# Shifted copies of two bias rows: from DRAM to DRAM by head on GpSimd's queue

## The chip, the core and the metric

The kernel runs on one core of a Trainium2 chip. The metric is the device time of one execution in microseconds (us). Before the change it is 3416.61 us, the median of 3 runs (3416.25 to 3418.32).

A core has five engines that run side by side and meet at semaphores: TensorE (PE, matmuls), VectorE (DVE), ScalarE (ACT), GpSimd (POOL) and SyncE (SP). Transfers are issued from queues, here SP's for the weights and GpSimd's for smaller things, and are carried by 16 DMA engines.

## The reference

Two transformer blocks over 512 tokens of 1024 channels. The first block has two layers, each a feed-forward, a mix of four kinds of attention and recurrence, and a second feed-forward; the second block has one layer of feed-forward, two attentions and feed-forward. Two of the attentions add a bias to the scores that depends only on the distance between query and key and on the head:

```python
def nsa_mixer(...):                      # first block, 4 heads, in both layers
    ...
    wl = einsum(qb, kwb) + t5_table[t5_bucket(wd)].transpose(2, 0, 1)
    o_w = einsum(masked_softmax(wl, wmask), vwb)
    ...

def dilated_window_attention(q, k, v, t5_bias, window, dilation):   # second block, 8 heads
    ...
    bias = t5_bias[:, t5_bucket_2(off * dilation)]
    s = where(valid, einsum(qs, k_blk) * HEAD_DIM ** -0.5 + bias[:, None], MASK_VALUE)
    ...
```

As the bias depends on the distance alone, a head needs one row of numbers, one for each distance. For 128 queries on 128 partitions the row is wanted 128 times, each copy shifted by one place.

## The kernel before, in words

Activations stay in SBUF, channels on partitions. All large products run in three passes on TensorE (`mm3`, lines 306 to 315): each operand is split in a high and a low part, and high x high (line 308), low x high (311) and high x low (312) are added up in PSUM. Weights come in chunks of 128 x 1024 (512 KB) through `wchunk` (lines 287 to 300): SP loads the chunk into one of four buffers named `raw` (line 289), ACT casts its halves into `hi` (line 296), VectorE subtracts to get `lo` (line 297). There are four buffers each for `hi` and `lo`, of half a chunk. A `raw` buffer is free for the next load when its second `lo` is made.

A feed-forward (`ffn`, line 669) turns through 22 pieces of its inner width. In each turn two chunks are loaded and multiplied (2 x 24 matmuls of 512 columns); ACT applies silu, VectorE multiplies into `u` (line 701), GpSimd makes the operands of the down projection, `uh` (line 708) and `ul` (line 711). These are read only after the 22 turns. In the first feed-forward of the kernel, loads for the modulation (`in_ada`, line 382) go through the same `raw` buffers and SP's queue.

The bias rows are made as a side work, given to `ffn` as the generator `side`: from the fourth turn on, one step of it is taken in each turn, between `uh` and `ul` (line 710). `setup_nsa` (line 521) runs in the first feed-forward of layer one, `setup_bias` (line 532) in the second feed-forward of layer two (weights `in_f2a`) and, for what is left, in the first feed-forward of the second block (`in_g1a`). Each makes its rows with a matmul against one-hot columns and then writes 128 equal copies of each row to a DRAM tensor: `nsa_d` of 4 x 128 x 640 (lines 529 and 530) and `dil_d` of 8 x 128 x 1024 (line 547), from 4 and 8 partitions of SBUF, on SP's queue, the one of the weights. The source of line 547, `lcd`, is itself a `raw` buffer (line 517). The attentions read `nsa_d` and `dil_d` back on GpSimd's queue with a row step of 639 and 1023 elements, which makes the shift (lines 1485 and 1710). `setup_bias` also prepares the table of the neighbourhood attention from DRAM to DRAM on GpSimd's queue: one broadcast `nrb_d` (line 534), three `t1_d` (538, shown as `t_d` in the rows), and 24 `nb_d` (551).

Instructions are emitted in the program's order and a scheduler sets the order on each engine; `dep(a, b)` adds that `a` stands behind `b`. DMA waits for what it reads and overwrites.

Of the kernel before, what the change touches and what calls it, by code (L numbers as in the profile page):

```python
# [9 lines left out]
F32 = mybir.dt.float32  # L10
# [17 lines left out]
# channel blocks of w_in that come out with channels on partitions, in the order they are computed  # L28
# [30 lines left out]
# columns of per-channel parameters  # L59
# [166 lines left out]
def _body(tc, nc, ctx, I, out):  # L226
# [16 lines left out]
    # ---- activation tables: the functions come in runs that one table serves  # L243
# [3 lines left out]
    def dep(a, b):  # L247
        tc.add_manual_dep(a.ins, b.ins.name, NOS, reason="table")
# [15 lines left out]
    # ---- small helpers  # L264
# [11 lines left out]
    class Parts(list):  # L276
        """columns in tiles of n"""
# [47 lines left out]
    # ---- constants and parameters  # L325
# [48 lines left out]
    # ---- conditioning: mod = silu(c) @ ada_w + ada_b, one third of a sublayer (1024 columns) at a time  # L374
# [36 lines left out]
    def mod_first():  # L411
        """the first norm, scale and shift, in two parts of the channels, with the first products between"""
# [96 lines left out]
    # ---- bias vectors of relative distances, kept in DRAM with one shifted copy per partition  # L509
    nsa_d = DR.tile([4, 128, 640], F32, name="nsa_d")  # L510
    dil_d = DR.tile([8, 128, 1024], F32, name="dil_d")
    nrb_d = DR.tile([16, 7680], F32, name="nrb_d")
# [8 lines left out]
    def setup_nsa():  # L521
        oh = bias_in("k_oh", 32, 640)
        yield
        r, ng = w_("r")[0:4], w_("ng")[0:4, 0:128]
        ps = psa()
        PE.matmul(ps[0:4, :], t5, oh[:, 0:512], start=True, stop=True)
        V.memset(ng, NEG)
        S.copy(r, ps[0:4, :])
        nc.sync.dma_start(nsa_d[:, :, 0:512], r.unsqueeze(1).to_broadcast([4, 128, 512]))
        nc.sync.dma_start(nsa_d[:, :, 512:640], ng.unsqueeze(1).to_broadcast([4, 128, 128]))  # L530

    def setup_bias():
        n = I["nrb"]
        i = nc.gpsimd.dma_start(nrb_d, bass.AP(n.tensor, n.offset, [[0, 16], [1, 7680]]))
        dep(i, order["ul"])
        for k, off in enumerate((0, -8, -16)):
            yield
            nc.gpsimd.dma_start(t1_d[k], bass.AP(nrb_d.tensor, nrb_d.offset + off + 31,
                                                 [[7679, 16], [960, 8], [64, 15], [1, 32]]))
        yield  # L540
        ohd, lcd = bias_in("k_ohd", 32, 1024), bias_in("k_lcd", 8, 1024)
        yield
        for h in range(2):
            ps = psa()
            PE.matmul(ps[0:8, :], t5b, ohd[:, h * 512:h * 512 + 512], start=True, stop=True)
            V.tensor_tensor(lcd[:, h * 512:h * 512 + 512], ps[0:8, :], lcd[:, h * 512:h * 512 + 512], op=ALU.add)
        nc.sync.dma_start(dil_d, lcd.unsqueeze(1).to_broadcast([8, 128, 1024]))
        yield
        for rr in range(8):
            for k in range(3):  # L550
                i = nc.gpsimd.dma_start(nb_d[:, rr * 16:rr * 16 + 16, k],
                                        t1_d[k, :, :, 7 - rr:15 - rr].rearrange("c h a b -> h c (a b)"))
                dep(i, order["ul"])
                yield

    # ---- norm over the channels of x, and the product's left operand in two parts
# [3 lines left out]
    class Stat:  # L560
        """(mean of the squares over the channels + EPS) ** -0.5 for each token, on all partitions"""
# [19 lines left out]
        def add_all(self):  # L581
            """of x, with the sums in two chains"""
            s = [self.s, self.r]
            p = self.p[0] = psa("st")
            for k in range(KD):
                q = s[k] if k < 2 else w_("sq")
                S.activation(q, xbox["x"][:, k], AF.Square)
                if 1 < k < KD - 1:
                    i = (V if k % 2 else G).tensor_tensor(s[k % 2], s[k % 2], q, op=ALU.add)
                    if k == 2:  # L590
                        dep(i, order["post"])
                    if k % 2 == 0:
                        order["aft"] = i
            for t in s:
                V.tensor_tensor(q, q, t, op=ALU.add)
            PE.matmul(p, ones, q, start=True, stop=True)
# [20 lines left out]
    def scaled(k, gain, sl):  # L617
        """x * gain; the norm's factor, the same for all channels of a token, is applied to the products"""
        xk, g = xbox["x"][:, k, sl], gain[:, k:k + 1]
        i = S.activation(hh[:, k, sl], xk, AF.Copy, scale=g)  # L620
        if sl.start == 0 and order["ev"]:
            dep(i, order["ev"][-1 if k >= KD // 2 else -2])
        run["cur"].append(i)
        V.scalar_tensor_tensor(hl[:, k, sl], xk, g, hh[:, k, sl].bitcast(F32), op0=ALU.mult, op1=ALU.subtract)  # L624

    # ---- A phase is a generator: it loads its first weights, multiplies them with each half of the tokens, does the
    # rest but its last products, and does these for each half; so the norm between two phases overlaps with both.
    evac = []

    def link(a, b, pre, early=False):  # L630
        """the end of phase a with the beginning of phase b; pre(h) makes half h of b's operand"""
# [15 lines left out]
    def first(ws):  # L647
        """the first chunks of a phase; needs the operand's tokens by halves"""
# [19 lines left out]
    # ---- feed-forward  # L668
# [70 lines left out]
    def wout_first(w, qs, cs, order, ns):  # L739
        """the first two chunks, with the parts ns of the contraction"""  # L740
# [52 lines left out]
    def rsq(o, i, scale, bias=None):  # L793
        """(scale * i + EPS) ** -0.5"""
        n = i.shape[0]
        act(o, i, AF.Ln, scale=scale, bias=epsc[0:n])
        act(o, o, AF.Exp, scale=-0.5)

    # ---- independent pieces of work are emitted in turn
# [12 lines left out]
    # ---- the four mixers of the first block  # L812
# [13 lines left out]
    def _mix1(l, MX, q0):  # L826
# [51 lines left out]
        def conv(t, v, n, cw):  # L878
            """causal depthwise convolution along the tokens"""
# [5 lines left out]
        # gated deltanet: short convolution and silu  # L885
# [17 lines left out]
        # compression of the keys and values of the first mixer  # L903
        hs = t_([128, 4, 32], "hs")

        def compress():
# [17 lines left out]
            # blocks as rows, those of the high parts and those of the low parts; the sum comes with the transpose  # L924
# [35 lines left out]
        # projections with tokens on partitions: values of the two others, and all gates  # L960
# [25 lines left out]
        # gates  # L986
# [6 lines left out]
        def softplus(o, xin, tmp):  # L993
            """o = max(xin, 0) + ln(1 + exp(-|xin|))"""
# [18 lines left out]
        def gates():  # L1013
            """silu and sigmoid of the output gates"""
# [31 lines left out]
    def sums(w, s, tiles):  # L1046
        """w^T s, in two passes with s in two parts, for a w of zeros and ones"""
# [33 lines left out]
    def gdn(blkr, l, MX, m_, n_, q_, s_, c_, t_, out_split, pr, cv, ga, beta, lvl):  # L1081
        kT, qT = [], []
        # decays
# [11 lines left out]
        # l2 norm of keys and queries  # L1095
# [15 lines left out]
        # (1 + B)^-1 by doubling the block size, for two heads at once: S keeps B of the head of parity 0, transposed, above  # L1111
        # the diagonal, and B of the other below. With X the lower inverse of the first head and Y the upper one of the
        # second's transpose, Z holds the blocks of X at even places and those of Y at odd places, and R the others.
# [3 lines left out]
        def sets(a, s):  # L1117
            """columns that stay in Z from a level to the next, and those that change places with R's"""
# [6 lines left out]
        # per chunk, heads in the order (parity, block)  # L1125
# [70 lines left out]
        # the recurrence over chunks  # L1196
# [81 lines left out]
    def mlstm(sel2, l, MX, m_, n_, q_, s_, c_, t_, out_split, pr, vd, gt, lf):  # L1278
        # running sums and maxima of the gates, heads on partitions; lf holds -log_sigmoid
# [84 lines left out]
    def soft_a(n_, s_, qh, kh, n, bias, nb=1):  # L1364
        """scores of 128 queries, exp(scores - max); the row sum comes with the values"""
# [12 lines left out]
    def soft_b(n_, t, n, o, vs):  # L1378
        """transpose of the weights, and their product with the values"""
# [11 lines left out]
    class Late:  # L1391
        """the second and third steps of a softmax, each some units behind the one before"""
# [18 lines left out]
    def nsa(blkr, l, MX, m_, n_, q_, s_, c_, t_, out_split, pr, hs, cw2, va, sg):  # L1411
        # compressed keys and values
# [22 lines left out]
        # norms of queries and keys  # L1435
# [46 lines left out]
        for h in range(4):  # L1482
# [3 lines left out]
            # compressed branch  # L1486
# [66 lines left out]
    # ---- the two attentions of the second block  # L1553
# [16 lines left out]
    def _mix2(MX, q0, wf):  # L1570
# [23 lines left out]
        # Scores take two passes: queries and keys in two parts each, high and low, and a product over the 128 rows  # L1594
        # (high, low) of a head's queries and (high, high) of its keys, then the high queries with the low keys.
# [190 lines left out]
    # ---- second block: residual with a norm after the product  # L1786
    gh = P.tile([128, 3, KD], F32, name="gh")

    def keep(g):
        """the product, scaled, in the place of x, which is in DRAM meanwhile"""  # L1790
# [7 lines left out]
    def post(h, gain=None):  # L1798
        """x += rmsnorm(y) * g, with y * g in the place of x; then the next phase's operand, or the end"""
# [24 lines left out]
    # ================================================================ program  # L1824
# [31 lines left out]
    def pre(h):  # L1856
        for k in range(KD):
            scaled(k, C("f1pre", 0, 8), HV[h])
# [25 lines left out]
```

## Time and profile before

| | |
|---|---|
| time, median of 3 | 3416.61 us |
| span of the profiled execution | 3414.4 us |
| PE busy | 3244.8 us (95%) |
| DVE busy | 1718.9 us (50%) |
| ACT busy | 1212.3 us (36%) |
| POOL busy | 732.8 us (21%) |
| weights' and SP's other transfers (q1) | 392.53 MB, 38.0% of 16 engines |
| GpSimd's transfers (q0) | 15.25 MB, 1.5% of 16 engines |

The span runs from the first to the last instruction of the profiled execution; the page gives no other time of it. Busy time counts instructions, and matmuls overlap, so PE's share says when PE had work, not how fast it did it. The share of a DMA queue is the time that its packets took, over 16 engines.

### The profile page before, as it was taken

The page shows a single profiled execution, that of the slowest core. Times are in us where ns is not written, and L with a number is a line of the kernel's source. Part 1 is how long each engine was busy: PE and PEld are TensorE (multiplying, and loading weights), DVE is VectorE, ACT ScalarE, POOL GpSimd, SP SyncE. Part 2 cuts the span into 40 slices and gives each one's busy share as a digit, 9 for nine tenths or more (in the row PEclk, how much of TensorE's full clock was granted, in tenths as well). Part 3 has the DMA queues.
Part 4 walks back from the last instruction along what each step waited for, and adds up shares of the span by engine and source line. Part 5 has one row for each costly group of instructions (what it writes and reads, how often), then busy time and mean ns, then how long its engine had stood idle before and what let it go on. Part 6 is the DMA issues. An engine that isn't in the chain of part 4 may idle for free.

```text
span 3414.4 us, 42938 instructions
## 1 busy us (share of the span) xinstructions
PE 3244.8 (95%) x16168; PEld 2690.2 (79%) x16168; DVE 1718.9 (50%) x2942; ACT 1212.3 (36%) x2287; POOL 732.8 (21%) x742
## 2 busy tenths in 40 slices
PE   7699999999999999999999992999999999999998
PEld 6488887778888888888777881888888877778887
DVE  6255576556555555537655530334443354554433
ACT  3122254454222232225445420233222345552232
POOL 3122222114222222212211420211221120131111
PEclk8899999999999999999999996999999999999999
DMA  6455642013555445534201335333333354443333
GB/s 229 106 177 162 194 147 89 29 41 129 166 167 168 152 150 173 158 116 143 87 29 41 114 106 73 115 107 109 110 103 95 106 170 114 116 125 98 99 96 103
DMA packets 133824, 410.73 MB, mean 120 GB/s; under 512 B 16073, under 2 KB 30025, under 8 KB 133345
## 3 DMA queue, kind: packets, MB, share of 16 engines
q1 hardware_dynamic: 128880, 392.53, 38.0%
q0 software_dynamic: 4592, 15.25, 1.5%
q8 instruction: 127, 2.08, 0.3%
q14 instruction: 81, 0.66, 0.1%
q10 hardware_dynamic: 144, 0.21, 0.0%
HBM read 374.07 MB, written 22.46 MB: 116 GB/s over the span
## 4 chain that ended last, share of the span: by engine, by line
PE 88%; DVE 4%; another core or an unknown queue 2%; DMA 2%; ACT 2%; issue 1%; POOL 1%; SPq 0%; DVEq 0%; ACTq 0%; POOLq 0%
PE m L308 14%; PE m L311 14%; PE m L312 14%; PE a L308 11%; PE a L312 11%; PE a L311 11%; PE o L1388 2%; PE pt L1382 1%; DMA raw<-in_f1a_dram 1%; DVE lo L297 1%; PE s L1700 1%; PE S L1328 1%; PE a L1182 1%; PE a L1166 1%
## 5 line engine op out<-in xcount | busy, mean ns | idle before, releaser
L297 DVE TENSOR_TENSOR lo<-raw,hi 128x512 fp32r<-128x512 f32 (+2 forms) x1056 | 803.6, 766 | 1008.2 <-ACT hi L296 985.5
L296 ACT CAST hi<-raw 128x512 fp32r<-128x512 f32 (+2 forms) x1056 | 638.7, 611 | 1742.6 <-PE m L311 885.7
L308 PE MATMUL m<-hh,hi 128*128 128x512 f32 (+1 forms) x1728 | 669.4, 387 | 78.0 <-ACT hi L296 66.8
L311 PE MATMUL m<-hl,hi 128*128 128x512 f32 (+1 forms) x1728 | 662.0, 383 | 5.6 <-DVE hl L624 4.3
L312 PE MATMUL m<-hh,lo 128*128 128x512 f32 (+1 forms) x1728 | 660.1, 382 | 1.7 <-DVE lo L297 1.7
L308 PE MATMUL a<-hh,hi 128*128 128x512 f32 (+1 forms) x1264 | 477.1, 377 | 32.9 <-ACT hi L296 32.9
L311 PE MATMUL a<-hl,hi 128*128 128x512 f32 (+1 forms) x1264 | 476.5, 377 | 1.0 <-DVE hl L614 1.0
L312 PE MATMUL a<-hh,lo 128*128 128x512 f32 (+1 forms) x1264 | 475.5, 376 | 0.0
L308 PEld LDWEIGHTS m<-hh,hi 128*128 128x128 f32 x1728 | 327.6, 190 | 141.6 <-ACT hi L296 67.3
L311 PEld LDWEIGHTS m<-hl,hi 128*128 128x128 f32 x1728 | 327.7, 190 | 66.8 <-DVE hl L624 5.4
L312 PEld LDWEIGHTS m<-hh,lo 128*128 128x128 f32 x1728 | 327.3, 189 | 64.9 <-DVE lo L297 5.6
L708 POOL TENSOR_SCALAR uh<-u 128x512 fp32r<-128x512 f32 x132 | 112.2, 850 | 1213.0 <-DVE u L701 820.9
L308 PEld LDWEIGHTS a<-hh,hi 128*128 128x128 f32 x1264 | 240.1, 190 | 76.2 <-ACT hi L296 33.8
L311 PEld LDWEIGHTS a<-hl,hi 128*128 128x128 f32 x1264 | 239.9, 190 | 44.8 <-DVE hl L614 1.8
L312 PEld LDWEIGHTS a<-hh,lo 128*128 128x128 f32 x1264 | 239.5, 189 | 43.5 <-DVE lo L297 1.0
L308 PE MATMUL a<-uh,hi 128*128 128x512 f32 (+1 forms) x660 | 229.6, 348 | 0.6
L311 PE MATMUL a<-ul,hi 128*128 128x512 f32 (+1 forms) x660 | 229.5, 348 | 0.0
L312 PE MATMUL a<-uh,lo 128*128 128x512 f32 (+1 forms) x660 | 228.7, 347 | 0.0
L308 PE MATMUL m<-uh,hi 128*128 128x512 f32 x528 | 205.8, 390 | 0.0
L312 PE MATMUL m<-uh,lo 128*128 128x512 f32 x528 | 205.4, 389 | 0.0
L311 PE MATMUL m<-ul,hi 128*128 128x512 f32 x528 | 205.4, 389 | 0.0
L711 POOL TENSOR_TENSOR ul<-u,uh 128x512 fp32r<-128x512 f32 x132 | 200.9, 1522 | 10.8
(460 smaller groups left out, 4002.1 us busy)
## 6 DMA issues: line engine op xcount, KB each, us to landing
raw<-in_ada_dram SPq DMA_DIRECT2D x144, 512.0 KB, 4.3
raw<-in_f1a_dram SPq DMA_DIRECT2D x88, 512.0 KB, 4.0
raw<-in_f2a_dram SPq DMA_DIRECT2D x88, 512.0 KB, 3.9
raw<-in_win_dram SPq DMA_DIRECT2D x48, 512.0 KB, 3.4
raw<-in_g1a_dram SPq DMA_DIRECT2D x44, 512.0 KB, 3.8
raw<-in_g2a_dram SPq DMA_DIRECT2D x44, 512.0 KB, 3.7
raw<-in_f1b_dram SPq DMA_DIRECT2D x32, 512.0 KB, 3.7
raw<-in_f2b_dram SPq DMA_DIRECT2D x32, 512.0 KB, 3.6
```

Source lines behind the costliest of these rows:

```text
L296: order["hi"] = S.copy(h, raw[:, s])
L297: order["lo"] = V.tensor_tensor(l, raw[:, s], h.bitcast(F32), op=ALU.subtract)
L308: i = PE.matmul(o, wh, xh, start=start, stop=False)
L311: PE.matmul(o, wh, xl, start=False, stop=False)
L312: j = PE.matmul(o, wl, xh, start=False, stop=stop)
L708: G.tensor_scalar(uh[:, j], u, 1.0, 0.0, op0=ALU.mult, op1=ALU.add)
L711: order["ul"] = G.tensor_tensor(ul[:, j], u, uh[:, j].bitcast(F32), op=ALU.subtract)
L1166: PE.matmul(p[:, bs_], B[:, bs_], Z[:, bs_], start=True, stop=True)
L1182: PE.matmul(p[:, bs_], RT[:, bs_], w[:, bs_], start=True, stop=True)
L1328: PE.matmul(ps[:, 0:n], dk[b][r, j * 128:j * 128 + 128], dq[b][r, j * 128:512], start=True, stop=True)
L1382: PE.transpose(pt[:, j * 128:j * 128 + 128], t[:, j * 128:j * 128 + 128], ident)
L1388: PE.matmul(o, r[:, j * 128:j * 128 + 128], v, start=j == 0, stop=j == len(vs) - 1)
```

## The change

Each row is first written once to a small DRAM tensor, `nsa_r` (4 x 640) or `dil_r` (8 x 1024), by SP. Then one transfer for each head, issued from GpSimd's queue, writes 128 copies of the row from there to `nsa_d[h]` (320 KB) or `dil_d[rr]` (512 KB). The four of `nsa_d` are issued one in each step of `side`, after one more empty step; the eight of `dil_d` stand ahead of every third `nb_d` transfer. Each stands behind the newest `ul`. The diff also takes out comments, which changes nothing; those parts are left out here.

```diff
@@ bias vectors of relative distances
     nsa_d = DR.tile([4, 128, 640], F32, name="nsa_d")
     dil_d = DR.tile([8, 128, 1024], F32, name="dil_d")
+    nsa_r = DR.tile([4, 640], F32, name="nsa_r")
+    dil_r = DR.tile([8, 1024], F32, name="dil_r")
...
@@ setup_nsa
         S.copy(r, ps[0:4, :])
-        nc.sync.dma_start(nsa_d[:, :, 0:512], r.unsqueeze(1).to_broadcast([4, 128, 512]))
-        nc.sync.dma_start(nsa_d[:, :, 512:640], ng.unsqueeze(1).to_broadcast([4, 128, 128]))
+        nc.sync.dma_start(nsa_r[:, 0:512], r)
+        nc.sync.dma_start(nsa_r[:, 512:640], ng)
+        yield
+        for h in range(4):
+            yield
+            i = nc.gpsimd.dma_start(nsa_d[h], nsa_r[h].unsqueeze(0).to_broadcast([128, 640]))
+            dep(i, order["ul"])
...
@@ setup_bias
-        nc.sync.dma_start(dil_d, lcd.unsqueeze(1).to_broadcast([8, 128, 1024]))
+        nc.sync.dma_start(dil_r, lcd)
         yield
         for rr in range(8):
+            i = nc.gpsimd.dma_start(dil_d[rr], dil_r[rr].unsqueeze(0).to_broadcast([128, 1024]))
+            dep(i, order["ul"])
             for k in range(3):
                 i = nc.gpsimd.dma_start(nb_d[:, rr * 16:rr * 16 + 16, k],
```

On SP, in the first feed-forward, the order before around the transfer of the rows `r` (`raw` are weight and modulation chunks):

```order
L289 DMA raw_850<-in_f1a_dram 128x1024
L289 DMA raw_890<-in_f1a_dram 128x1024
L529 DMA nsa_d<-r_802 512x1x512
L382 DMA raw_925<-in_ada_dram 128x1024
L289 DMA raw_928<-in_f1a_dram 128x1024
L382 DMA raw_963<-in_ada_dram 128x1024
```

and with the change, where its line is 531:

```order
L289 DMA raw_852<-in_f1a_dram 128x1024
L289 DMA raw_892<-in_f1a_dram 128x1024
L382 DMA raw_927<-in_ada_dram 128x1024
L531 DMA nsa_r<-r_804 4x512
L289 DMA raw_930<-in_f1a_dram 128x1024
L382 DMA raw_965<-in_ada_dram 128x1024
```

The transfer writes the row tensor instead of the copies, and one modulation load has come ahead of it.

On GpSimd, in the second feed-forward of layer two, the order before from the first `nb_d` transfer on:

```order
L551 DMA nb_d<-t_d 8x16x256
L708 TENSOR_SCALAR uh_16590<-u_17352 128x512
L711 TENSOR_TENSOR ul_16591<-u_17352,uh_16590 128x512
L551 DMA nb_d<-t_d 8x16x256
L708 TENSOR_SCALAR uh_16590<-u_17428 128x512
L711 TENSOR_TENSOR ul_16591<-u_17428,uh_16590 128x512
L551 DMA nb_d<-t_d 8x16x256
L708 TENSOR_SCALAR uh_16590<-u_17504 128x512
L711 TENSOR_TENSOR ul_16591<-u_17504,uh_16590 128x512
```

and with the change, where `uh`, `ul` and `nb_d` have the lines 717, 720 and 560:

```order
L560 DMA nb_d<-t_d 8x16x256
L717 TENSOR_SCALAR uh_16596<-u_17358 128x512
L720 TENSOR_TENSOR ul_16597<-u_17358,uh_16596 128x512
L560 DMA nb_d<-t_d 8x16x256
L557 DMA dil_d<-dil_r 128x1024
L717 TENSOR_SCALAR uh_16596<-u_17435 128x512
L720 TENSOR_TENSOR ul_16597<-u_17435,uh_16596 128x512
L560 DMA nb_d<-t_d 8x16x256
L717 TENSOR_SCALAR uh_16596<-u_17511 128x512
L720 TENSOR_TENSOR ul_16597<-u_17511,uh_16596 128x512
L557 DMA dil_d<-dil_r 128x1024
L560 DMA nb_d<-t_d 8x16x256
```

The first two copies of `dil_d` now stand there; five of the eight lie in this feed-forward and three in the next. On TensorE no instruction moves.

## Rows read from the trace of the kernel before

**Rows 1.** Page, the span in 40 equal slices of 85.4 us: busy tenths, DMA share, GB/s.
```profile
PE   7699999999999999999999992999999999999998
...
DMA  6455642013555445534201335333333354443333
GB/s 229 106 177 162 194 147 89 29 41 129 166 167 168 152 150 173 158 116 143 87 29 41 114 106 73 115 107 109 110 103 95 106 170 114 116 125 98 99 96 103
```

**Rows 2.** Waits, 2020 to 2140: who waited for whom, us in total, times, longest.
```profile
ACT hi L296 <- DMA raw<-in_f2a_dram: 71.1, 2, 70.9
```

**Rows 3.** Timeline of PE about the later gap: start, duration, instruction, idle before it.
```profile
2062.02 0.39 PE L308 MATMUL a<-hh,hi 128*128 128x512 f32 x1
...
2065.20 0.39 PE L312 MATMUL a<-hh,lo 128*128 128x512 f32 x1
2132.43 0.80 PE L308 MATMUL m<-hh,hi 128*128 128x512 f32 x1 [66.84 <-ACT hi L296]
...
2137.72 0.39 PE L311 MATMUL m<-hl,hi 128*128 128x512 f32 x1
```

**Rows 4.** Timeline of PE about the earlier gap.
```profile
133.13 0.39 PE L312 MATMUL m<-hh,lo 128*128 128x512 f32 x1
166.46 0.79 PE L308 MATMUL a<-hh,hi 128*128 128x512 f32 x1 [32.95 <-ACT hi L296]
...
172.16 0.39 PE L308 MATMUL a<-hh,hi 128*128 128x512 f32 x1
```

**Rows 5.** Timeline of ACT at the end of the earlier gap.
```profile
165.79 1.14 ACT L296 CAST hi<-raw 128x512 fp32r<-128x512 f32 x2 [31.64 <-DMA raw<-in_f1a_dram]
```

**Rows 6.** SP's DMA issues about both places.
```profile
118.78 0.67 SPq L529 DMA_DIRECT2D nsa_d<-r  x1
...
2044.40 0.77 SPq L547 DMA_DIRECT2D dil_d<-raw  x1
```

**Rows 7.** Windows: us, busy time of five engines, clock, DMA share, GB/s.
```profile
60.00:90.00 30.00, 30.00 (x134) 24.86 (x133) 18.12 (x20) 9.35 (x16) 8.60 (x7) 1.00 0.56 178
150.00:160.00 10.00, 0.00 (x0) 0.00 (x0) 0.00 (x0) 0.00 (x0) 0.00 (x0) 0.50 0.23 25
1970.00:1972.00 2.00, 2.00 (x10) 1.68 (x9) 0.46 (x1) 1.12 (x2) 0.00 (x0) 1.00 0.96 264
2100.00:2110.00 10.00, 0.00 (x0) 0.00 (x0) 0.00 (x0) 0.00 (x0) 0.00 (x0) 0.50 0.47 50
```

**Rows 8.** SP's waits, 2020 to 2140.
```profile
SPq L289 <- DMA dil_d<-raw: 38.7, 1, 38.7
```

**Rows 9.** DMA issues: times, KB each, median us to landing.
```profile
dil_d<-raw SPq DMA_DIRECT2D x1, 4096.0 KB
...
nsa_d<-r SPq DMA_DIRECT2D x1, 1024.0 KB
...
nrb_d<-in_nrb_dram POOLq DMA_DIRECT2D x1, 480.0 KB, 4.4
```

**Rows 10.** Timeline of POOL about both places.
```profile
121.38 1.29 POOL L711 TENSOR_TENSOR ul<-u,uh 128x512 fp32r<-128x512 f32 x1
128.96 0.63 POOL L708 TENSOR_SCALAR uh<-u 128x512 fp32r<-128x512 f32 x1 [6.29 <-DVE u L701]
...
1968.75 0.55 POOL L534 DMA_DIRECT2D nrb_d<-in_nrb_dram  x1
...
2044.98 0.68 POOL L551 DMA_DIRECT2D nb_d<-t_d  x1
2055.60 0.99 POOL L708 TENSOR_SCALAR uh<-u 128x512 fp32r<-128x512 f32 x1 [9.95 <-DVE u L701]
```

**Rows 11.** One line: issues of the existing transfers on GpSimd's queue, duration in ns.
```profile
L551 POOL DMA_DIRECT2D nb_d<-t_d x24: 644/644/722, 2034.1 to 2511.9; - x24
```

**Rows 12.** Tiles: the readers of the two tensors, first and last start.
```profile
L1485 POOL DMA_DIRECT2D md<-nsa_d x8: 577/584/598, 570.8 to 1791.7; - x8
...
L1710 POOL DMA_DIRECT2D md<-dil_d x8: 536/537/564, 2750.1 to 2870.9; - x8
```

## The prediction

> **What bounds the kernel now.** I read the span in slices first. PE is at nine tenths in almost every slice; the exceptions are the first slice (7), the second, 85 to 171 us (6), and the twenty-fifth, 2049 to 2134 us, where PE falls to 2 and the transfer rate drops to 73 GB/s [rows 1]. So the kernel is bound by matmuls, and a change off TensorE can win only where PE stands still. The waits around that slice name the cause: ACT, which turns each weight chunk into its high part, waited once for 70.9 us on a weight transfer [rows 2], and PE's own timeline shows the gap that followed, 66.84 us up to 2132.43 [rows 3]. A second gap of 32.95 us ends at 166.46 [rows 4], and there too ACT's cast before it waited on a weight transfer, 31.64 us [rows 5]. Then I asked what stood on the weights' queue before either gap: at 118.78 the score bias for the first block's attention goes out (line 529), at 2044.40 the one for the dilated attention (line 547) [rows 6].
>
> The windows inside the gaps show what these two transfers do. With nothing but them left to move, the sixteen DMA engines are busy 0.23 of the time at 25 GB/s in the first gap and 0.47 at 50 GB/s in the second [rows 7]: 0.23 x 16 is about 4 engines and 0.47 x 16 about 8, one for each head, each at some 6.2 GB/s. 1024 KB at 25 GB/s takes 42 us, 4096 KB at 50 GB/s takes 84 us [rows 9]; counted from their issue they end at about 161 and 2128, just before PE moves again at 166.46 and 2132.43. In the second place SP also waited 38.7 us for the transfer itself, because its source is one of the four weight buffers [rows 8].
>
> **What is removed.** The two broadcast transfers leave SP. What comes in their place moves each row once: 4 x 2 KB and 4 x 512 B, and 8 x 4 KB. At the 6.2 GB/s per engine of the old form a 4 KB row takes 0.7 us, so SP's queue and the weight buffer are free again within a few us, and the weights behind have nothing to wait for. Matmul starts lie 0.227 us apart at full clock (2062.02 to 2065.20 is 14 steps) [rows 3]. Gap one, start to start: 166.46 - 133.13 - 0.23 = 33.1 us. Gap two: 2132.43 - 2065.20 - 0.23 = 67.0 us. [...] Sum: 33.1 + 67.0 + 1.6 + 1.7 = 103.4 us.
>
> **What is added, and what hides it.** Twelve transfers from DRAM to DRAM on GpSimd's queue, 4 of 320 KB and 8 of 512 KB. Issuing one costs GpSimd about what its other transfers cost, 0.64 us [rows 11]: 12 x 0.64 = 7.7 us, on an engine that in each turn of the loop waits for VectorE (6.29 and 9.95 us) [rows 10]. A turn is 48 matmuls, 10.9 us. GpSimd's products of a turn are read only in the down projection, so nothing waits for them there. The first of the four stands behind the products that end at 121.38 + 1.29 = 122.67 and now waits for the row that SP sends at about 119 to 120; if that takes 3 us GpSimd waits under 1 us, and its next product is due at 128.96 [rows 10]. The readers come at 570.8 and 2750.1 [rows 12], hundreds of us after the last copy, which by the order stands some turns into the next feed-forward.
>
> The transfers themselves share the 16 DMA engines with the weights. No row shows this very form. The slow bound takes the 6.2 GB/s per engine of the old form on 16 engines, 100 GB/s: 3.3 us for 320 KB, 5.2 for 512 KB. The fast bound takes the best rate in a window, 264 GB/s [rows 7]: 1.2 and 2.0 us. The nearest row is the broadcast that GpSimd's queue already makes from DRAM to DRAM, 16 copies of 30 KB (480 KB), landed in 4.4 us with PE at full rate [rows 7, 9, 10]; I take that, 2.9 and 4.7 us with the wait for the landing in it. The cover is shown by the old transfers themselves: with the weights held up from 118.78 on, PE ran until 133.36, 14.6 us; from 2044.40 until 2065.43, 21.0 us [rows 3, 4, 6]. A delay of 5 us stays under either. It is also won back before the next: at a DMA share of 0.56 a turn of 10.9 us leaves 4.8 us of every engine idle in the first place [rows 7], and more in the second, where the slices show threes and fours [rows 1]. So I cost the added transfers at 0, in both bounds. If that cover were gone, each would cost its whole time: 4 x 3.3 + 8 x 5.2 = 55 us. What the transfers could gain beyond that is nothing: PE is full outside the two gaps.
>
> The order of a few casts and additions on ACT and VectorE moves by a few places around line 529 and line 547; PE's order does not move. Each such instruction is under 1.3 us and VectorE waits in those stretches, so I cost it at 0, within 1 us either way.
>
> **The sum.** The page gives no time of its profiled execution beside the span, 3414.4 us; the median of the runs is 3416.61, 2.2 us above. Span after: 3414.4 - 103.4 = 3311.0. Time after: 3416.6 - 103.4 = 3313.2 us.
>
> **Rivals.** *The copies collide with the weights.* For it: in the first place loads for the modulation run on the same queue and engines are busy 0.56 of the time. Against it: the cover of 14.6 and 21.0 us. With the four copies of the first place uncovered at the slow bound the gain is 103.4 - 13 = 90 us, 3326; with all twelve, 103.4 - 55 = 48 us, 3368.
>
> *The queue is changed, the weights still wait.* If the new copies ran on the same few engines at the same rate, the same bytes would block the same engines for 42 and 84 us in sum, in pieces of 42 / 4 and 84 / 8, both 10.5 us. Back to back they act as one transfer does now, and the time is 3416.6; a turn or more apart, as the order has them, each stays under its cover and the time is the forecast's. For it: the DMA engines are the same ones. Against it: the 16-row broadcast above, 480 KB in 4.4 us, where four engines at 6.2 GB/s would need 19 us.
> [...]
>
> *The copies go narrow and the kernel gets slower.* Each copy has one source row; if the source row set the spread, one engine would carry 512 KB at 6.2 GB/s in 84 us, past a cover of 21.0, and 320 KB in 53 us past 14.6. Stalls: 8 x 63 + 4 x 38 = 656 us, against 103 won: about 3970. It decides from the number of engines: with two, 8 x 21 + 4 x 12 = 216 us lost and 113 net, about 3530; with four or more the stalls fall to nearly nothing and the gain stands. Against it: both sides of the copy have 128 rows, and the 4.4 us transfer has one source row too.
> [...]
>
> **How the numbers follow.** Forecast 0.86; collisions 0.08; queue changed but weights still waiting 0.03; narrow 0.03. About 0.2%, 7 us, is what a measurement of this kernel tells from no change. Faster by more than that: 0.86 + 0.08 = 0.94; within it 0.03; slower 0.03. The range: below the forecast 2 us of spread between runs, 1 us of reordered work and 3 us in which a gap hid other small waits of PE, 3307; above it, the first form of the collision and 2 us of spread, 3328. What lies outside holds the rest of the collisions and the other two rivals, about 0.15.
>
> **What would show it.** Right: no PE gap over a few us at 120 to 170 or in the second feed-forward of the second layer; clock 1.00 throughout there; DMA share up by about 0.1 to 0.2 in those windows but none at 0.23 or 0.47 with 25 or 50 GB/s; the copies landed within 3 to 7 us. Collisions would show as PE waits on casts of 1 to 5 us, each just after a copy's issue. Wide or narrow is read from the DMA share during a copy. I am wrong if a gap stays whose releaser is a cast waiting on a weight transfer, or if GpSimd's products come so late that the down projection waits for them.

## The result, and the profile after

| | before | after |
|---|---|---|
| median of the timed runs | 3416.43 us (3415.6 to 3418.32) | 3315.8 us (3313.13 to 3317.06) |
| span of the profiled execution | 3414.4 us | 3311.4 us |
| PE busy | 3244.8 us (95%) | 3242.6 us (98%) |

There are four runs of each; the forecast was worked out from the first three before, median 3416.61 us. The ratio is 0.9703, with a 95% interval of 0.9689 to 0.9716. The profiled execution after took 3313.13 us beside its span of 3311.4. The forecast was 3313.2 with a range of 3307 to 3328, and a span of 3311.0.

The page of the kernel after, in the same slices as [rows 1] (here of 82.8 us each):

```profile
PE   7999999999999999999999999999999999999998
...
GB/s 235 183 167 173 175 143 72 33 45 139 167 168 165 154 143 176 164 117 132 111 34 30 109 100 134 120 118 105 128 97 98 135 148 118 99 139 97 96 94 104
```

Both dips of PE are gone: the second slice has 9 and not 6, the twenty-fifth 9 and not 2. The second slice moves 183 GB/s where it moved 106, and the twenty-fifth 134 where it moved 73.

Next, windows of the kernel after where the two gaps lay; columns as in [rows 7]:

```profile
120.00:150.00 30.00, 30.00 (x134) 24.86 (x133) 15.38 (x18) 8.43 (x15) 7.63 (x8) 1.00 0.68 220
150.00:180.00 30.00, 30.00 (x138) 24.93 (x137) 15.87 (x22) 7.74 (x14) 8.20 (x7) 1.00 0.48 161
2020.00:2060.00 40.00, 40.00 (x179) 33.10 (x178) 12.77 (x19) 11.39 (x19) 12.04 (x13) 1.00 0.37 119
2060.00:2100.00 40.00, 40.00 (x178) 33.14 (x177) 12.52 (x19) 10.85 (x18) 11.52 (x13) 1.00 0.37 121
```

PE is busy throughout at a granted clock of 1.00; nowhere does the DMA share stand at 0.23 or 0.47 with 25 or 50 GB/s beside an idle PE, as in [rows 7]. The rise of the DMA share by 0.1 to 0.2 that the prediction named came in the first place (0.68, where 60 to 90 us of the same execution has 0.53) and not in the second (0.37, as from 2140 to 2180 us, where no copy is on the way). The longest waits of PE in the whole execution after (who waited for whom, us in total, times, longest):

```profile
PE st L586 <- ACT sq L582: 7.2, 6, 2.0
PE a L422 <- ACT sq L421: 6.4, 1, 6.4
PE m L308 <- ACT hh L474: 5.3, 2, 3.9
```

There is no wait on a cast `hi` among them; those behind [rows 3, 4], of 66.84 and 32.95 us, were the two longest. ACT's longest wait on a weight chunk in the first place is 2.4 us instead of 31.64 [rows 5], and in the second place SP's wait for its own transfer is 1.6 us instead of 38.7 [rows 8]. The twelve copies themselves, as DMA issues (columns as in [rows 9]):

```profile
dil_d<-dil_r POOLq DMA_DIRECT2D x8, 512.0 KB, 4.9
...
nsa_d<-nsa_r POOLq DMA_DIRECT2D x4, 320.0 KB, 4.5
```

They land in 4.9 and 4.5 us, where the prediction estimated 4.7 and 2.9. A window in which hardly anything but one copy of `dil_d` and one small transfer of `nb_d` is on the way shows that the copies go wide:

```profile
2036.00:2038.00 2.00, 2.00 (x10) 1.66 (x9) 0.69 (x1) 1.12 (x2) 0.00 (x0) 1.00 0.70 211
```

The share of 0.70 is the time of eleven engines, more than the eight of before. Issuing a copy costs GpSimd less than the 0.64 us of [rows 11], here by line with the least, the median and the most in ns:

```profile
L536 POOL DMA_DIRECT2D nsa_d<-nsa_r x4: 557/560/584, 120.6 to 153.6; - x4
...
L557 POOL DMA_DIRECT2D dil_d<-dil_r x8: 547/587/587, 2012.8 to 2387.2; - x8
```

So the time came from where the forecast looked for it. What the two traces leave open is why. The change does four things at once: it moves the copies to another queue, splits them by head, spaces them out, and reads them from DRAM instead of from a few SBUF partitions. My theory was the spread: few DMA engines at 6.2 GB/s each before, all sixteen after. The rivals were the queue, the spacing, and the source.

### The profile page after: what moved, and what is told of

Its sections match the earlier page's. It is cut to its first block, busy times and chain, and to the rows that moved or that the text cites. A ratio compares the mean times of both kernels' runs of the same rounds, so it can differ in the third digit from the quotient of the medians.

```text
span 3311.4 us, 42958 instructions
## 1 busy us (share of the span) xinstructions
PE 3242.6 (98%) x16168; PEld 2690.1 (81%) x16168; DVE 1723.8 (52%) x2942; ACT 1212.6 (37%) x2287; POOL 740.8 (22%) x754
## 4 chain that ended last, share of the span: by engine, by line
PE 91%; DVE 5%; ACT 2%; issue 1%; POOL 1%; DMA 1%; SPq 0%; DVEq 0%; ACTq 0%; POOLq 0%
PE m L308 14%; PE m L311 14%; PE m L312 14%; PE a L308 11%; PE a L312 11%; PE a L311 11%; PE o L1397 2%; PE pt L1391 2%; DVE lo L297 1%; PE s L1709 1%; PE S L1337 1%; PE a L1191 1%; PE a L1175 1%; PE s L1533 1%; PE num L1343 1%
## 5 line engine op out<-in xcount | busy, mean ns | idle before, releaser
L311 PEld LDWEIGHTS m<-hl,hi 128*128 128x128 f32 x1728 | 327.4, 189 | 66.5 <-DVE hl L633 5.4
L720 POOL TENSOR_TENSOR ul<-u,uh 128x512 fp32r<-128x512 f32 x132 | 203.1, 1538 | 10.8
```

Of the source, the lines that this page charges most:

```text
L311: PE.matmul(o, wh, xl, start=False, stop=False)
L720: order["ul"] = G.tensor_tensor(ul[:, j], u, uh[:, j].bitcast(F32), op=ALU.subtract)
```

## The experiments

Each kernel computes the whole reference. The diffs are against the kernel after, but for `e3_queue_only` and `e8_own_buffer`, which are against the kernel before. Ratios are to runs of the kernel before on the same chip, with 95% intervals. PE's instructions stand in the same order as before in all of them but `e3_queue_only` and `e6_sbuf_by_head`, where 108 and 512 of the 16168 stand elsewhere.

**One place at a time.** `e1_nsa_only` keeps the old transfer of `dil_d`, `e2_dil_only` the old ones of `nsa_d`:

```diff
# e1_nsa_only
-        nc.sync.dma_start(dil_r, lcd)
+        nc.sync.dma_start(dil_d, lcd.unsqueeze(1).to_broadcast([8, 128, 1024]))
...
-            i = nc.gpsimd.dma_start(dil_d[rr], dil_r[rr].unsqueeze(0).to_broadcast([128, 1024]))
-            dep(i, order["ul"])
```
```diff
# e2_dil_only
-        nc.sync.dma_start(nsa_r[:, 0:512], r)
...
-            i = nc.gpsimd.dma_start(nsa_d[h], nsa_r[h].unsqueeze(0).to_broadcast([128, 640]))
-            dep(i, order["ul"])
+        nc.sync.dma_start(nsa_d[:, :, 0:512], r.unsqueeze(1).to_broadcast([4, 128, 512]))
+        nc.sync.dma_start(nsa_d[:, :, 512:640], ng.unsqueeze(1).to_broadcast([4, 128, 128]))
```

> Only the first block's bias (nsa_d) is made the new way; dil_d is written as before. If the two gaps are independent, as the sum of the prediction has it, the first gap (33.1 us and 1.6 us of slow clock) goes and the second of 67 us stays: 3416.4 - 34.7 = 3381.7 us, a ratio of 0.990. Rival, the gaps are coupled (by buffers or by the order of work): anything else, such as 3416 or 3350.

> Only the dilated attention's bias (dil_d) is made the new way; nsa_d is written as before. Independent gaps: the second gap (67.0 and 1.7 us) goes, the first stays: 3416.4 - 68.7 = 3347.7 us, a ratio of 0.980. Rival, coupled gaps: the two single gains do not add up to the 100.6 us of both.

Measured: 3382.60 us, 0.9904 (0.9888 to 0.9921), and 3348.77 us, 0.9803 (0.9788 to 0.9818). PE's longest wait in either, `e1_nsa_only` first:

```profile
PE m L308 <- ACT hi L296: 66.8, 1, 66.8
```
```profile
PE a L308 <- ACT hi L296: 33.6, 1, 33.6
```

Each leaves the other's gap as it was. Against 3415.28 for the kernel before in the same set of runs they win 32.7 and 66.5 us, 99.2 together; the whole change won 100.6. The two places are independent, and the terms of the sum stand.

**The queue alone.** `e3_queue_only` is the kernel before with its old transfers issued by GpSimd:

```diff
-        nc.sync.dma_start(nsa_d[:, :, 0:512], r.unsqueeze(1).to_broadcast([4, 128, 512]))
-        nc.sync.dma_start(nsa_d[:, :, 512:640], ng.unsqueeze(1).to_broadcast([4, 128, 128]))
+        for o, i in ((nsa_d[:, :, 0:512], r.unsqueeze(1).to_broadcast([4, 128, 512])),
+                     (nsa_d[:, :, 512:640], ng.unsqueeze(1).to_broadcast([4, 128, 128]))):
+            dep(nc.gpsimd.dma_start(o, i), order["ul"])
...
-        nc.sync.dma_start(dil_d, lcd.unsqueeze(1).to_broadcast([8, 128, 1024]))
+        dep(nc.gpsimd.dma_start(dil_d, lcd.unsqueeze(1).to_broadcast([8, 128, 1024])), order["ul"])
```

> The transfers of the kernel before, heads outermost and read from SBUF, moved to GpSimd's queue; nothing else is changed. Theory A, the form is what counts (few engines at 6.2 GB/s each, whatever queue feeds them): the weights' pieces on those 4 and 8 engines wait as before, both gaps stay at about 33 and 67 us, 3410 to 3420. Theory B, the queue counts (an engine takes turns between two queues): on a blocked engine a weight chunk's 32 KB are 8 pieces of 4 KB, each behind one 4 KB piece of 0.66 us, 8 x 0.85 = 6.8 us for a chunk where PE takes 5.44; PE falls behind by 1.4 us a chunk, over 84 us about 12 chunks or 17 us, less than the cover of 21: gaps of 0 to 10 us, 3315 to 3330.

Measured: 3359.0 us, 0.9834 (0.982 to 0.9849). Neither time came. PE's waits on casts, the two transfers, and a window while the second runs:

```profile
PE m L308 <- ACT hi L296: 15.9, 2, 14.9
PE a L308 <- ACT hi L296: 13.7, 5, 7.1
```
```profile
dil_d<-raw POOLq DMA_DIRECT2D x1, 4096.0 KB, 91.1
...
nsa_d<-r POOLq DMA_DIRECT2D x1, 1024.0 KB, 48.6
```
```profile
2070.00:2080.00 10.00, 10.00 (x46) 8.24 (x45) 3.19 (x5) 2.78 (x5) 1.76 (x3) 1.00 0.59 125
```

The transfers are no faster: 91.1 and 48.6 us, against the 84 and 42 worked out for before. But now 125 GB/s flow while one runs, with PE busy. With the same transfer on the weights' own queue it was 50 in most of the gap [rows 7] and 102 at the most, with PE idle:

```profile
2080.00:2090.00 10.00, 0.00 (x0) 0.00 (x0) 0.00 (x0) 0.00 (x0) 0.00 (x0) 0.50 0.64 102
```

What differs is when a weight load lands. Here are the times from issue to landing (least, median, most), first for the loads issued from 2080 to 2087 us in the kernel before, behind the transfer, then for the twelve issued while it runs in `e3_queue_only`, with their first and last start:

```profile
DMA to landing us min/median/max: 47.6/50.1/52.6
```
```profile
L289 SPq DMA_DIRECT2D raw<-in_f2a_dram x12: 327/328/328, 2042.0 to 2117.2; - x12
...
DMA to landing us min/median/max: 12.5/17.1/23.5
```

On the transfer's own queue a load landed only after the transfer's end. From the other queue loads landed while it ran, though in some 17 us where the median of these weights before is 3.9. Twelve loads over 75.2 us are one in 6.8 us, the rate of theory B, and PE takes a chunk in 5.44. What B had wrong is the gaps: 0 to 10 us were expected, and PE waits 18.9 us on casts in the first place and 10.8 in the second. PE's order is another one only from the end of these waits on (174.97 and 2115.93 us). The queue alone wins 56 us, somewhat over half.

**The form alone.** `e4_form_on_sp` leaves the copies by head from DRAM, but on SP, the weights' queue:

```diff
-            i = nc.gpsimd.dma_start(nsa_d[h], nsa_r[h].unsqueeze(0).to_broadcast([128, 640]))
-            dep(i, order["ul"])
+            nc.sync.dma_start(nsa_d[h], nsa_r[h].unsqueeze(0).to_broadcast([128, 640]))
...
-            i = nc.gpsimd.dma_start(dil_d[rr], dil_r[rr].unsqueeze(0).to_broadcast([128, 1024]))
-            dep(i, order["ul"])
+            nc.sync.dma_start(dil_d[rr], dil_r[rr].unsqueeze(0).to_broadcast([128, 1024]))
```

> The form of the change (a row in DRAM, one copy by head with 128 rows on both sides) but all issued on SP, the weights' queue; the scheduler puts one to four copies between two weight loads. Theory A, the form counts: each copy takes 3.8 to 6.3 us on 16 engines, bunches of four stay at the cover of 21 us, 3315 to 3335. Theory B, the queue counts: the copies, 5.25 MB in all, stand in front of the weights as before and both gaps come back for the most part, 3390 to 3416.

Measured: 3313.59 us, 0.9701 (0.9687 to 0.9716): all of the gain, with no wait on `hi` among PE's longest. The copies land after 8.0 us instead of 4.9, as the row of DMA issues has it, and PE does not feel it:

```profile
dil_d<-dil_r SPq DMA_DIRECT2D x8, 512.0 KB, 8.0
```

So GpSimd's queue is enough for half and needed for none. Something in the form made the transfers fast.

**The engines.** `e5_dram_narrow_sp` reads DRAM but keeps the old shape, one transfer with the heads outermost, on SP:

```diff
-        for h in range(4):
-            yield
-            i = nc.gpsimd.dma_start(nsa_d[h], nsa_r[h].unsqueeze(0).to_broadcast([128, 640]))
-            dep(i, order["ul"])
+        yield
+        nc.sync.dma_start(nsa_d, nsa_r.unsqueeze(1).to_broadcast([4, 128, 640]))
...
-            i = nc.gpsimd.dma_start(dil_d[rr], dil_r[rr].unsqueeze(0).to_broadcast([128, 1024]))
-            dep(i, order["ul"])
+            if rr == 0:
+                nc.sync.dma_start(dil_d, dil_r.unsqueeze(1).to_broadcast([8, 128, 1024]))
```

> The rows are first written to DRAM as in the change, but then one transfer on SP makes all copies, with the heads outermost (4 and 8), as before the change. If the few engines are the cause and 6.2 GB/s is what an engine does in such a broadcast: 1280 KB on 4 engines 52 us, 4096 KB on 8 engines 84 us, gaps of about 38 and 63 us, 3415 to 3425. If the slow part is the source in a single SBUF partition, an engine reading DRAM does 11 to 17 GB/s (the rate of the new copies and of weights): 20 to 29 us and 32 to 47 us, gaps of 5 to 14 and 11 to 26 us, 3330 to 3356.

Measured: 3317.9 us, 0.9715 (0.9687 to 0.9744). My theory expected the whole gain to vanish and falls here. The other time, 3330 to 3356 us, missed too, as it gave an engine that reads DRAM 11 to 17 GB/s. The windows in the middle of each transfer show it:

```profile
2018.00:2020.00 2.00, 2.00 (x10) 1.65 (x10) 0.00 (x1) 0.62 (x1) 0.00 (x0) 1.00 0.50 205
124.00:126.00 2.00, 2.00 (x10) 1.66 (x9) 1.14 (x2) 0.62 (x1) 0.00 (x0) 1.00 0.26 104
```

The share is that of 8 and of 4 engines, as in [rows 7], but the rate is four times as high: 205 / 8 and 104 / 4 are both 26 GB/s for an engine, not 6.2. The few engines were there before and are there now; what was slow before was not the engine. At 205 GB/s, 4096 KB take some 20 us, just under the cover of 21.0.

**The source.** `e6_sbuf_by_head` issues the eight copies of `dil_d` by head as the kernel after does, but each from the one SBUF partition that holds the row (`lcd` in a buffer of its own):

```diff
-        nc.sync.dma_start(dil_r, lcd)
...
-            i = nc.gpsimd.dma_start(dil_d[rr], dil_r[rr].unsqueeze(0).to_broadcast([128, 1024]))
+            i = nc.gpsimd.dma_start(dil_d[rr:rr + 1], lcd[rr:rr + 1].unsqueeze(1).to_broadcast([1, 128, 1024]))
```

> As the kernel after, but the eight copies of dil_d read their row from one SBUF partition instead of DRAM, one transfer by head with 128 rows on the destination, on GpSimd's queue; the rows stand in a buffer of their own. If 6.2 GB/s is the limit of an engine and the transfer spreads over 16: 5.2 us each, 3313 to 3320. If 6.2 GB/s is the limit of one source partition, or the transfer stays on one engine: 84 us each, beyond the cover of 21 by 63, eight times 500 us, about 3820, or less by as much as the weights pass on another queue; a DMA share of 16 engines or of one (0.06) during a copy tells these two apart.

Measured: 3340.82 us, 0.9783 (0.9754 to 0.9811), about 25 us above the kernel after. Its DMA row and a window within one copy:

```profile
dil_d<-lcd POOLq DMA_DIRECT2D x8, 512.0 KB, 21.0
```
```profile
2024.00:2028.00 4.00, 4.00 (x19) 3.30 (x19) 0.72 (x2) 0.74 (x2) 0.51 (x1) 1.00 0.96 28
```

All sixteen engines are busy, 0.96, and move 28 GB/s together. 512 KB in 21.0 us is 25 GB/s, whoever carries them. Neither expectation came whole: the transfer spreads over sixteen engines, as the first had it, and is held by its one source partition, as the second had it, but at 25 GB/s and not at 6.2. At 0.96 each moves under 2 GB/s: a busy engine is here, as I read it, one that waits for its source.

Each copy takes as long as its cover, and the 25 us are not the price of the copies alone. PE waits for nothing behind the first two. From 2077 us on the scheduler has put some of PE's work in another order, and the waits that were added are mostly not on weights; the largest, and all those on casts:

```profile
PE m L308 <- DVE g L713: 10.5, 4, 3.3
...
PE a L308 <- ACT hi L296: 2.2, 5, 0.5
```

The first copy shows one thing more: its issue, and two of the weight loads that SP issued while it was on the way:

```profile
2013.57 0.55 POOL L557 DMA_DIRECT2D dil_d<-lcd  x1
```
```profile
L289 SPq DMA_DIRECT2D raw<-in_f2a_dram x2: 328/4090/7851, 2018.4 to 2024.1; - x2
...
DMA to landing us min/median/max: 13.0/15.3/17.5
```

The copy landed at 2034.6, the loads at 2035.9 and 2037.1. The window's 28 GB/s leave them next to nothing beside the copy's 25. Here weights did not pass a slow transfer, though it was on another queue; it held all sixteen engines, and the one in `e3_queue_only` eight.

**The spacing.** `e7_back_to_back` issues all copies of a place in a row:

```diff
+        yield
         for h in range(4):
-            yield
...
+        for rr in range(8):
             for k in range(3):
```

> As the kernel after, but the four copies of nsa_d and the eight of dil_d are issued one right after the other. If spacing is needed (the prediction's collision rival): 4 MB at about 110 GB/s hold the engines for 38 us, the weights get through late, and what exceeds the cover of 21 us is lost, 10 to 20 us, 3325 to 3336. If the engines take turns between the two queues, a weight chunk takes at most twice its 3.9 us, under two chunks' 10.9 us of PE work with four buffers: nothing is lost, 3313 to 3318.

Measured: 3316.23 us, 0.9711 (0.9682 to 0.9739), no different from the kernel after. The window in the middle of the eight:

```profile
2026.00:2030.00 4.00, 4.00 (x19) 3.30 (x19) 1.38 (x2) 1.54 (x3) 0.00 (x0) 1.00 1.02 397
```

The weights are counted in. From issue to landing the eight copies took (least, median, most):

```profile
DMA to landing us min/median/max: 6.3/12.8/19.2
```

Even the slowest stays under the 21.0 us of cover, and no wait on a cast is among PE's longest. Spacing isn't needed, and the collisions that I gave 0.08 don't come even when they are provoked.

**The cover.** Two runs test how a gap follows from a transfer. `e8_own_buffer` is the kernel before with `lcd` in a buffer of its own, so that the transfer no longer holds one of the four weight buffers:

```diff
-        ohd, lcd = bias_in("k_ohd", 32, 1024), bias_in("k_lcd", 8, 1024)
+        ohd, lcr = bias_in("k_ohd", 32, 1024), bias_in("k_lcd", 8, 1024)
+        lcd = P.tile([128, 1024], F32, tag="acc", bufs=1, name="lcd")[0:8]
```

and `e9_half_from_sbuf` makes 64 of the 128 copies in the old way and the others from DRAM:

```diff
+        nc.sync.dma_start(dil_d[:, 0:64], lcd.unsqueeze(1).to_broadcast([8, 64, 1024]))
...
-            i = nc.gpsimd.dma_start(dil_d[rr], dil_r[rr].unsqueeze(0).to_broadcast([128, 1024]))
+            i = nc.gpsimd.dma_start(dil_d[rr, 64:128], dil_r[rr].unsqueeze(0).to_broadcast([64, 1024]))
```

> The kernel before, with the dilated rows in a buffer of their own, not in one of the four weight buffers; both transfers as before. If what holds PE up is the engines alone, the 38.7 us for which SP waited on the transfer's source cost nothing, but a fourth weight buffer can run one chunk (5.4 us) further ahead: the second gap shrinks from 67 to about 62 us, 3410 us. If the held buffer is a cause of its own, the gap shrinks by far more, to some 28 to 45 us, 3377 to 3394.

> As the kernel after, but half of the copies of dil_d (64 of each row) are written by one transfer on SP from the 8 SBUF partitions, as before the change, and the other 64 by head from DRAM on GpSimd's queue. If the gap is the transfer's time less a fixed cover of 21 us: 2048 KB at 50 GB/s take 42 us, and with the 4 us between the transfer's end and PE's start in the kernel before the gap is 42 - 21 + 4 = 25 us, with the slow clock behind it 27 us over the kernel after: about 3343 us. If the gap is in proportion to the bytes: 33.5 us and 1.7, 3351 us.

Measured: 3418.96 us, 0.9998 (0.9988 to 1.0007), and 3340.92 us, 0.9775 (0.9758 to 0.9791). PE's wait and SP's in `e8_own_buffer`, then PE's in `e9_half_from_sbuf`:

```profile
PE m L308 <- ACT hi L296: 66.9, 1, 66.9
...
SPq L289 <- DMA raw<-in_f2a_dram: 32.7, 1, 32.7
```
```profile
PE m L308 <- ACT hi L296: 25.4, 1, 25.4
```

Both expectations for the first missed. SP's wait of 38.7 us for the transfer [rows 8] turned into one of 32.7 us for weights, and PE's gap stayed: the loads that could now be issued lay behind the same transfer and did not land any sooner. The held buffer cost nothing. The second came as the cover has it: 2048 KB at 50 GB/s are 42 us, of which 21 are covered; with some 4 us from the landing to the first matmul, as in [rows 3], 25 are left, and 25.4 were seen.

**Where the rows lie.** Three runs keep SBUF as the source and one transfer on SP, and change only the partitions. `e10_sbuf_128` puts each row on 16 partitions and reads all 128; `e11_every_4th` puts the eight rows on partitions 0, 4, ... 28, `e12_every_2nd` on 0, 2, ... 14 (`lw` is loaded from `dil_r` by GpSimd):

```diff
# in place of the eight copies; e10_sbuf_128
+        lw = P.tile([128, 1024], F32, tag="acc", bufs=1, name="lw")
+        i = nc.gpsimd.dma_start(lw, bass.AP(dil_r.tensor, dil_r.offset, [[1024, 8], [0, 16], [1, 1024]]))
+        dep(i, order["ul"])
+        yield
+        nc.sync.dma_start(dil_d.rearrange("h (c r) w -> (h c) r w", r=8), lw.unsqueeze(1).to_broadcast([128, 8, 1024]))
# e11_every_4th; e12_every_2nd has [0:16:2]
+        lw = P.tile([128, 1024], F32, tag="acc", bufs=1, name="lw")[0:32:4]
+        i = nc.gpsimd.dma_start(lw, dil_r)
+        dep(i, order["ul"])
+        yield
+        nc.sync.dma_start(dil_d, lw.unsqueeze(1).to_broadcast([8, 128, 1024]))
```

> As the kernel after, but dil_d is written by one transfer on SP from SBUF, as before the change, with its source on 128 partitions: each of the 8 rows is first spread to 16 partitions (512 KB, from DRAM on GpSimd's queue), and each partition is then read 8 times. If what is slow is the few engines and partitions of the source, 16 engines read 16 times as many partitions: at 25 GB/s an engine, as with a DRAM source, 4096 KB take 10 to 14 us, under the cover of 21, and the time is the kernel's after, 3313 to 3318. If any repeated read of one SBUF row holds an engine at 6.2 GB/s, 16 engines do 100 GB/s: 42 us, a gap of 42 - 21 + 4 = 25 us, about 3341.

> As the kernel after, but dil_d is written by one transfer on SP, heads outermost, from 8 SBUF partitions that lie four apart (0, 4, ... 28) instead of side by side; the rows come there from DRAM by a transfer of 32 KB on GpSimd's queue. Theory A, one engine gets 6.2 GB/s from one SBUF partition: 8 engines, 50 GB/s, 84 us, the second gap is back, about 67 us, 3383. Theory B, four neighbouring partitions share one way out of some 25 GB/s (4 partitions gave 25, 8 gave 50, one partition read by 16 engines gave 25 to 28): 8 ways, 200 GB/s or what 8 engines do, 21 us, a gap of 21 - 21 + 4 = 0 to 5 us, 3315 to 3322.

> The same with the 8 rows on every second partition (0, 2, ... 14). Theory A: 50 GB/s, 84 us, a gap of about 67 us, 3383. Theory B: two rows for each group of four, 4 groups, 100 GB/s, 42 us, a gap of 42 - 21 + 4 = 25 us and 1.7 us of slow clock, about 3343.

Measured: 3314.72 us, 0.969 (0.9674 to 0.9706); 3315.69 us, 0.9706 (0.9691 to 0.972); 3333.56 us, 0.9756 (0.974 to 0.9773). A window within the transfer of each, in the same order:

```profile
2032.00:2034.00 2.00, 2.00 (x10) 1.65 (x10) 1.23 (x2) 0.62 (x1) 0.45 (x1) 1.00 1.02 416
```
```profile
2038.00:2042.00 4.00, 4.00 (x19) 3.34 (x18) 0.69 (x1) 1.12 (x2) 0.00 (x0) 1.00 0.51 183
```
```profile
2050.00:2060.00 10.00, 0.00 (x0) 0.00 (x0) 0.00 (x0) 0.00 (x0) 0.00 (x0) 0.52 0.49 99
```

SBUF as such isn't slow: with 128 partitions as the source the window has 416 GB/s, weights counted in, and the 4096 KB land after 13.7 us. Of the two runs with eight rows, the engines are the same eight (0.51 and 0.49), and the rate goes with the distance of the rows: 50 GB/s side by side [rows 7], 99 two apart, 183 four apart, close to the 205 that the eight engines took from DRAM. That is what one gets if four neighbouring partitions share 25 GB/s: eight rows lie in two, four and eight such fours. The third run kept a gap, 17.6 us instead of the 25 expected:

```profile
2047.74 0.39 PE L312 MATMUL m<-hh,lo 128*128 128x512 f32 x1
2065.70 0.80 PE L308 MATMUL a<-hh,hi 128*128 128x512 f32 x1 [17.58 <-ACT hi L296]
```

The rate came as expected; the cover did not. Here the transfer is issued at 2017.91 and PE runs until 2048, 30 us, since the loads were further ahead than at the place of line 547. 42 us less 30, and the 4 to 6 from landing to matmul, make the gap. In `e11_every_4th` the same step leaves PE a wait of 1.25 us.

No version beats the kernel after: `e4_form_on_sp`, `e7_back_to_back`, `e10_sbuf_128` and `e11_every_4th` (3313.59 to 3316.23) lie within its own runs.

## Why the prediction was right, and where it was not

- **Two gaps, 33.1 + 67.0 us, and the slow clock after them, 1.6 + 1.7.** Right: the span fell by 103.0 us where 103.4 were forecast, which is luck in part, as the profiled execution after was the fastest of the four. The places taken singly gave 32.7 and 66.5 us between medians. The medians differ by 100.6, 2.8 less, about the 3.9 us over which the runs after spread. No run parts the 1.6 and 1.7 us from the gaps; they are read from the trace before. The granted clock there is still 0.50 from 166.46 to 169 and from 2132.43 to 2135 us, and 1.00 from 172 and from 2138 us on; the matmul eighteen behind the first starts 5.70 us after it in the one place and the one sixteen behind it 5.29 in the other [rows 3, 4], where steps of 0.227 us make 4.09 and 3.63.
- **The copies cost nothing.** Right: PE waits for no cast behind them, though the four of `nsa_d` land in 4.5 us where I had estimated 2.9, above even the slow bound of 3.3, which had no wait for the landing in it. Against a cover of 14.6 us that decides nothing.
- **The cover.** Right as an idea, and `e9_half_from_sbuf` confirms the 21.0 us in numbers. It is not a constant: where the transfer is issued elsewhere, as in `e12_every_2nd`, it was 30 us.
- **GpSimd, 0.64 us for each issue.** 0.56 and 0.59 us; its products stay on time.
- **"About 4 engines and about 8, one for each head, each at some 6.2 GB/s."** The counts are right, the reason is wrong. The step took the rate of a transfer, divided it by its engines, and kept the quotient as a property of the engine. `e5_dram_narrow_sp` shows the same 4 and 8 engines at 26 GB/s each; `e6_sbuf_by_head` shows sixteen engines at under 2 each. What stayed the same in the slow runs was about 25 GB/s for each four neighbouring partitions of the source: 25 for four and 50 for eight side by side, 99 for eight two apart; eight four apart gave 183, 23 for each four. The slow bound of 100 GB/s and the 55 us without cover rest on that quotient, and so does the third rival.
- **"The queue is changed, the weights still wait"** (0.03) was argued away by the 16-row broadcast. `e3_queue_only` is the better answer: the slow transfers got no shorter, 91.1 and 48.6 us, and the weights went past, one chunk in 6.8 us; the queue alone won 56 us. `e6_sbuf_by_head` is another case: a copy on sixteen engines at 28 GB/s let neither of two loads issued while it was on the way land before it did.
- **"The copies go narrow"** (0.03), priced at about 3970 us. `e5_dram_narrow_sp` is narrow, with 4 and 8 engines, and takes 3317.9. In `e6_sbuf_by_head` sixteen engines got no more out of one partition, 25 GB/s, than four engines got out of four neighbours before; a copy from DRAM on a single engine wasn't tried.

That the forecast came out although its reason for the slow transfers was wrong has a plain cause: the sum needed only that the new copies stay under 14.6 and 21.0 us, and the row of a broadcast of the same kind (DRAM to DRAM, 480 KB in 4.4 us, [rows 9]) said so by itself. Two things stay open. In `e3_queue_only` PE still waits 29.6 us on casts: a load landed in some 17 us, and only three `raw` buffers were free for loads while the transfer held the fourth as its source; whether a fourth would have brought a chunk more often than each 6.8 us no run here shows. And why weights pass a slow transfer there and not in `e6_sbuf_by_head` isn't shown: the two differ in the engines held, in the source partitions of one transfer and in its size.

## What to carry to other kernels

Where PE stands still and the trace shows DMA engines busy at a low rate (here 0.47 at 50 GB/s), ask what the engines wait for before counting them: divide the rate by the source's partitions as well as by the engines. A transfer cost here its length less the work that was already loaded ahead of it: in `e9_half_from_sbuf` 42 us less 21, and some 4 to the first matmul, for a gap of 25.4. Bring it under that cover: with a source in DRAM (205 GB/s on eight engines) or rows four partitions apart (183) the runs came to 3313.59 to 3317.9 us, whatever the queue, the split or the spacing. If it can't be made faster, issuing it on another queue than the weights' may save part: 56 of 100.6 us here, with eight of the sixteen engines held, but weights did not pass a copy that held all sixteen (28 GB/s, two loads landed after 13.0 and 17.5 us).

## What the runs showed of the hardware that was not expected

- Eight rows of 4 KB, read 128 times by 8 engines, move at 50, 99 and 183 GB/s when they lie on neighbouring, every second and every fourth partition, and at 205 GB/s from DRAM.
- A single partition read by sixteen engines gives 25 GB/s (512 KB in 21.0 us) with the engines busy 0.96 of the time. The DMA share alone doesn't tell a full queue from a starved one: 0.96 stands beside 28 GB/s there, 1.02 beside 397 in `e7_back_to_back`.
- From DRAM to DRAM, or from 128 partitions, sixteen engines move 397 and 416 GB/s, with the weights that pass in that window counted in, beside a PE at full clock.
- The loads of the weights `in_f2a` take 3.9 us in the median. Behind a slow transfer on their own queue two landed after 47.6 and 52.6 us, when the transfer was over; with the transfer on GpSimd's queue and eight engines after 12.5 to 23.5 us, while it ran; beside a copy on GpSimd's queue and sixteen engines after 13.0 and 17.5 us, just behind the copy's end.
